# Seven transform tiles in the conv mixer, and an even layer that multiplies by a normalised operand

## The chip, the cores and the metric

The kernel runs on one core of a Trainium2 chip. The time is the device time of one execution in microseconds (us); lower is better. A core has a matrix engine (TensorE, PE in the rows; its weight loads are PEld), VectorE (DVE), ScalarE (ACT), GpSimd (POOL) and SyncE (SP), which issues the DMAs. Each engine works off its own instructions in program order and waits on semaphores for the others.

## The reference, cut to what matters

Four layers and two MLPs over 512 tokens of width 1024, in fp32. The change touches three of the stages.

```python
def conv_mixer(h, w_pw1, b_pw1, w_dw, b_dw, ln_g, ln_b, w_pw2, b_pw2):
    a = h @ w_pw1 + b_pw1
    u = a[..., :D_MODEL] * sigmoid(a[..., D_MODEL:])
    u = causal_depthwise_conv(u, w_dw) + b_dw          # 31 taps
    u = silu(layernorm(u, ln_g, ln_b))
    return u @ w_pw2 + b_pw2

def even_layer(x, norm_pre, norm_post, w_in, conv_w, conv_b, gate_w, gate_b, lam, sc_w, w_out):
    h = rmsnorm_2(x, norm_pre)
    xa, za, xb, gb, gc, zb = split(h @ w_in)           # six blocks of 1024 columns
    ua = centred_dwconv(xa, conv_w, 2) + conv_b        # 4 taps
    ya = rg_lru(ua, ..., False) + rg_lru(ua, ..., True)
    ya = ya * silu(za)
    yb = gb * centred_dwconv(gc * xb, sc_w, 1)         # 3 taps
    yb = yb * silu(zb)
    y = concatenate([ya, yb]) @ w_out
    return x + rmsnorm_2(y, norm_post)
```

The third is the start of the odd layer (`odd_layer`, gated linear attention): its decay gates are `log_sigmoid` of a product with a narrow low-rank projection.

## The kernel before, in words

**Layout.** Activations lie transposed: 8 tiles of 128 channels by 512 tokens (`h[:, k, :]`). Every product is made of three fp32r matmuls: an operand x is kept as XH (rounded) and XL = x - XH, a weight chunk of 128x1024 as `whi` and `wlo` likewise, and `mac` (L146 to L149) multiplies hi by XH, hi by XL and lo by XH. A *chunk* is one weight chunk against eight operand tiles, 24 matmuls into one PSUM bank.

**Weights.** `weights(ahead)` takes the next chunk and calls `split_to`, which for each chunk up to `ahead` further on issues a DMA on SP into one of four staging tiles, rounds it on ACT (`whi`, L101) and subtracts on the engine in `st["lo"]` (`wlo`, L102): DVE, except where the program sets POOL. It does so in the conv mixer from its first chunk on.

**Background work.** `chunk` calls `step` after every second k; `step` advances generators in the list `bg`, so that transforms, norms and recurrences are issued in slices between matmuls. What a generator issues stands in PE's, DVE's and ACT's queues in just that place.

**Conv mixer.** `a` is computed in 16 chunks: for each of the eight channel tiles m a gate chunk (`gate_half`) and a linear chunk (`lin_half`), which yields `u` (L749, L753). The first five m use all tokens; the last three are run in two halves of 256 tokens. The 31-tap convolution goes two ways. Tiles m < DIRECT (two) run `direct`: 31 instructions on DVE (L719, L721), a few per hook. The other six run `conv` once per half: three transposes on PE (`uT`, L676), a forward transform (`re`, L682), two products with the filter's spectrum on DVE (`pq`, L688), 12 inverse matmuls (`cv`, L696). YU, YA and YB say how many hooks lie between these steps. `centre` subtracts the mean of the first transform tile (`lns`) on DVE and adds sums on POOL (L664, L667). When all tiles of a half are done, `norm(half)` forms the layer norm (`lnm`), and `ln_a` to `ln_d` make XH and XL for the second product, `kouter2` (tile `ko`), one step per PACE[half] hooks.

**Even layer.** XZ is the order of the first 16 chunks (x is the recurrent branch, z its gate); then for each m the four chunks gc, xb, gb, zb. The operand is h times the gains `gfe`, without the norm's factor `rs2` (which `comb_a` and `comb_b` bring out of the sums while the first chunks run), so each result is multiplied by `rs2` behind its chunk: xa on DVE (L1077), za on DVE (L1084), the gc*xb product by `rq` = rs2 squared (L1101), yb on POOL (L1107), zb on DVE (L1121). `rg(m)` is the recurrence of tile m: `taps` (L975, L977), `halves`, four gate products, Tanh, Exp and Sqrt on ACT, two scans on DVE, and sums on POOL (L1022, L1028, L1049, L1050). It runs in the background, a step per half chunk pair, over all 48 chunks. Then `wob` and `woa` are the two halves of the output product.

**Odd layer.** `decays` (a generator) scales the low-rank projection, rounds it (`lrs`, L1331 to L1333), waits two hooks and issues the gate products `z` (L1343, L1344) between the chunks of `v`.

Of the kernel before, what the change touches and what calls it, by code (L numbers as in the profile page):

```python
# [7 lines left out]
F32 = mybir.dt.float32  # L8
F32R = mybir.dt.float32r
# [5 lines left out]
P = 128  # L15
NT = 512
# [31 lines left out]
def tile_model(ctx, tc, xT, wall, gwall, vecs, opost, wglr, bglr, wdw, dft, out):  # L48
# [14 lines left out]
    RGH, XAB, DCH, HDH, TKH, FIN = 0.5, 6, 2, 1.3, 1.5, 0.8  # L63
# [87 lines left out]
    def chunk(o, xh, xl, hook=0, wt=None, ks=range(KD), ns=slice(0, NT)):  # L151
# [465 lines left out]
    with ExitStack() as e:  # L617
# [51 lines left out]
        def conv(m, u, half, lag=0):  # L669
# [15 lines left out]
            for i in range(2):  # L685
                q = cp.tile([P, NW], F32, tag="pq", name="pq", bufs=4)
# [114 lines left out]
        PACE = (2, 1)  # L801
# [26 lines left out]
        st["lo"] = [pool]  # L828
        for c in range(10):
            m = c // 2  # L830
            if c == 7:
# [67 lines left out]
    with ExitStack() as e:  # L899
        ep = e.enter_context(tc.tile_pool(name="even", bufs=1))  # L900
        tmp_pool[:] = [ep, 6]
        sz = ep.tile([P, KD, NT], F32, name="sz")
        yb = ep.tile([P, KD, NT], F32, name="yb")
        rq = ep.tile([P, NT], F32, name="rq")
# [66 lines left out]
        def taps(m):  # L971
# [3 lines left out]
            dve.tensor_scalar(u, xa[:, 0:NT], vec[:, w0:w0 + 1], V("rcb", m), op0=ALU.mult, op1=ALU.add)  # L975
# [11 lines left out]
        def rg(m):  # L987
# [11 lines left out]
            for d in range(2):  # L999
                for g in range(2):  # L1000
# [6 lines left out]
                    s = gp.tile([P, NT], F32, tag="ri", name="ri", bufs=5)  # L1007
# [65 lines left out]
        def put_xa(m, o):  # L1073
# [3 lines left out]
            dve.tensor_tensor(out=xa[:, 2:NT + 2], in0=o, in1=rs2, op=ALU.mult)  # L1077
# [730 lines left out]
```

## Time and profile before

| | us |
|---|---|
| three runs | 1835.55, 1841.36, 5206.65 |
| their median | 1841.36 |
| the profiled execution | 1839.13 |
| its span, first to last instruction | 1837.4 |

| engine | busy us | share of the span |
|---|---|---|
| PE | 1790.3 | 97% |
| PEld | 1490.2 | 81% |
| DVE | 1036.1 | 56% |
| ACT | 795.9 | 43% |
| POOL | 519.1 | 28% |

PE is the engine that sets the time nearly everywhere: of the chain that ended last 80% lies on PE, 12% on DVE. The profile's forty slices show where it is not so: the row of PE has 8 in place of 9 in two neighbouring slices around 720 to 780 us, in one near 1400 us, and in the last third near 1580 us; in the row of the granted clock one slice (the second of the two in the conv mixer) has 8 in place of 9. To read the rows below: a row of the windows view gives for each engine its busy time and, in brackets, how many instructions it ran; PEclk is the mean clock that PE was granted, as a share of 2.4 GHz, the upper of its two levels (the lower is 1.2 GHz). In a row of the timeline the two first numbers are the start and the duration, xN says how many instructions in a row were merged, and the bracket at its end says how long the engine stood idle before it and for whom.

### The profile page before, as it was taken

Reading aid. Unit: us, or ns where it says so; the run is one execution under the profiler, and the core shown is the slowest. Engines: PE = TensorE matmul, PEld = TensorE weight load, DVE = VectorE, ACT = ScalarE, POOL = GpSimd, SP = SyncE. Lnnn points to the kernel's source line nnn. Section 1 sums busy time; section 2 is a strip of 40 time slices with the busy share of each in tenths; the row PEclk is TensorE's granted clock in tenths of the full one; section 3 lists DMA queues with packets and bytes.
Section 4 is the critical chain, followed back from the end, with each engine's and each line's share of the span. In section 5 each row is a group of like instructions: output and inputs, shape, how many; then the busy total and the mean of one; then the engine's idle time right before and its main releaser. Section 6 shows DMA issues by size and latency. Waiting matters only on the chain.

```text
span 1837.4 us, 22578 instructions
## 1 busy us (share of the span) xinstructions
PE 1790.3 (97%) x8762; PEld 1490.2 (81%) x8762; DVE 1036.1 (56%) x1457; ACT 795.9 (43%) x1234; POOL 519.1 (28%) x411
## 2 busy tenths in 40 slices
PE   9999999999999998899999999999998999999998
PEld 7778878888888877798888888888876878878887
DVE  5796544333334579865333334767878843745354
ACT  5334444332423433465332424545565644446553
POOL 1333322010202345535010201413434303552230
PEclk9999999999999999899999999999999999999999
DMA  5222113222223322112323223232222233222121
GB/s 189 69 80 73 59 54 103 95 99 96 93 100 101 101 73 91 46 47 81 98 94 101 91 98 104 80 115 101 84 80 92 81 103 103 70 87 81 47 69 47
DMA packets 45931, 159.68 MB, mean 87 GB/s; under 512 B 5217, under 2 KB 6625, under 8 KB 45824
## 3 DMA queue, kind: packets, MB, share of 16 engines
q1 hardware_dynamic: 45824, 158.24, 25.8%
q8 instruction: 69, 1.13, 0.3%
q14 instruction: 38, 0.31, 0.1%
HBM read 156.13 MB, written 2.10 MB: 86 GB/s over the span
## 4 chain that ended last, share of the span: by engine, by line
PE 80%; DVE 12%; ACT 4%; issue 2%; DMA 1%; POOL 1%; SPq 0%; DVEq 0%; ACTq 0%; POOLq 0%
PE w L148 12%; PE w L149 12%; PE w L147 12%; DVE y L721 2%; PE ko L148 1%; PE ko L149 1%; PE ko L147 1%; DVE wlo L102 1%; DVE ua L977 1%; PE k L147 1%; PE lg L467 1%; PE o L499 1%; PE v L441 1%; PE q L149 1%; PE q L147 1%
## 5 line engine op out<-in xcount | busy, mean ns | idle before, releaser
L102 DVE TENSOR_TENSOR wlo<-stg,whi 128x1024 fp32r<-128x1024 f32 x231 | 308.5, 1337 | 251.0 <-ACT whi L101 249.9
L101 ACT ACTIVATE whi<-stg 128x1024 fp32r<-128x1024 f32 x284 | 297.8, 1051 | 232.6 <-PE w L148 125.3
L596 POOL TENSOR_TENSOR UL<-u,UH 128x512 fp32r<-128x512 f32 x64 | 83.4, 1303 | 514.5 <-ACT UH L595 514.5
L148 PE MATMUL w<-XL,whi 128*128 128x512 f32 (+1 forms) x520 | 200.6, 386 | 0.0
L147 PE MATMUL w<-XH,whi 128*128 128x512 f32 (+1 forms) x520 | 200.6, 386 | 0.0
L149 PE MATMUL w<-XH,wlo 128*128 128x512 f32 (+1 forms) x520 | 200.6, 386 | 0.0
L148 PE MATMUL w<-UL,whi 128*128 128x512 f32 x512 | 199.4, 389 | 0.1
L147 PE MATMUL w<-UH,whi 128*128 128x512 f32 x512 | 199.2, 389 | 0.0
L149 PE MATMUL w<-UH,wlo 128*128 128x512 f32 x512 | 199.2, 389 | 0.0
L102 POOL TENSOR_TENSOR wlo<-stg,whi 128x1024 fp32r<-128x1024 f32 x53 | 130.7, 2473 | 158.7 <-ACT whi L101 158.4
L260 POOL TENSOR_TENSOR sacc<-sacc,sq 128x512 f32<-128x512 f32 (+1 forms) x57 | 71.2, 1256 | 181.2 <-ACT sq L259 180.9
L149 PEld LDWEIGHTS w<-XH,wlo 128*128 128x128 f32 x520 | 97.7, 188 | 19.7
L148 PEld LDWEIGHTS w<-XL,whi 128*128 128x128 f32 x520 | 97.7, 188 | 19.6
L147 PEld LDWEIGHTS w<-XH,whi 128*128 128x128 f32 x520 | 97.7, 188 | 19.6
L148 PEld LDWEIGHTS w<-UL,whi 128*128 128x128 f32 x512 | 96.1, 188 | 20.8 <-POOL UL L596 0.9
L149 PEld LDWEIGHTS w<-UH,wlo 128*128 128x128 f32 x512 | 96.1, 188 | 19.9
L147 PEld LDWEIGHTS w<-UH,whi 128*128 128x128 f32 x512 | 96.1, 188 | 20.0
L594 DVE TENSOR_TENSOR u<-relu 128x512 f32<-128x512 f32 x64 | 45.4, 710 | 104.5 <-ACT relu L592 104.5
L592 ACT ACTIVATE relu<-w 128x512 f32<-128x512 f32 x64 | 38.2, 597 | 151.0 <-PE w L149 151.0
L147 PE MATMUL ko<-XH,whi 128*128 128x256 f32 x256 | 74.4, 290 | 3.5 <-ACT XH L823 3.5
L604 DVE TENSOR_TENSOR acc<-w,acc 128x512 f32<-128x512 f32 x32 | 22.1, 692 | 97.1 <-PE w L149 97.1
L148 PE MATMUL ko<-XL,whi 128*128 128x256 f32 x256 | 73.7, 288 | 2.3 <-DVE XL L252 2.2
(469 smaller groups left out, 4201.1 us busy)
## 6 DMA issues: line engine op xcount, KB each, us to landing
stg<-wall SPq DMA_DIRECT2D x284, 512.0 KB, 3.3
gst<-gwall SPq DMA_DIRECT2D x4, 512.0 KB, 3.6
h<-xT SPq DMA_DIRECT2D x3, 512.0 KB, 5.8
out<-yo SPq DMA_DIRECT2D x6, 256.0 KB, 2.1
stg<-wall SPq DMA_DIRECT2D x8, 128.0 KB, 4.8
h<-xT SPq DMA_DIRECT2D x2, 256.0 KB, 3.8
ex<-wglr SPq DMA_DIRECT2D x2, 256.0 KB, 3.8
sacc<-opost SPq DMA_DIRECT2D x2, 256.0 KB, 4.4
```

Of the source, the lines that this page charges most:

```text
L101: act.activation(hi, src, AF.Copy)
L102: eng.tensor_tensor(out=lo, in0=src, in1=hi, op=ALU.subtract)
L147: pe.matmul(o, lhsT=hi[:, w], rhs=xh[:, k, ns], start=first, stop=False)
L148: pe.matmul(o, lhsT=hi[:, w], rhs=xl[:, k, ns], start=False, stop=False)
L149: pe.matmul(o, lhsT=lo[:, w], rhs=xh[:, k, ns], start=False, stop=last)
L260: eng.tensor_tensor(out=acc, in0=acc, in1=t, op=ALU.add)
L441: pe.matmul(acc[t], lhsT=XH[:, k, xs], rhs=wh, start=k == 0, stop=False)
L592: act.activation(r, o, AF.Relu)
L594: dve.tensor_tensor(out=u, in0=r, in1=r, op=ALU.mult)
L596: pool.tensor_tensor(out=UL[:, m, :], in0=u, in1=UH[:, m, :], op=ALU.subtract)
L604: dve.tensor_tensor(out=a, in0=o, in1=a, op=ALU.add)
L721: dve.scalar_tensor_tensor(o, src, w(j), o, op0=ALU.mult, op1=ALU.add)
```

## The change

- **Conv mixer.** DIRECT goes from 2 to 1: tile 1 is now a transform tile, and the pivot of `centre`. YB goes from (3, 3) to (4, 3): the inverse matmuls of the tiles m < 5 come one hook later; `pq` has six buffers in place of four. PACE goes from (2, 1) to (1, 1). The two settings of `st["lo"]` to POOL ahead of the second half are gone, so lo splits run on DVE until then. A new argument `mid` of `chunk` calls a function behind k = 3: the look-ahead split moves there from the chunk's start.
- **Even layer.** A new order SEQ; the first RAW = 7 chunks multiply by XH, XL as before. In the middle of chunks 3 to 6 `normal` makes NH, NL, the split of h*gfe*rs2, for two tiles each; all later chunks multiply by these, and their results need no rs2. The scalings listed above fall away with `rq` and `yb`; the first taps of both convolutions move from DVE to ACT; the sigmoid and product of z move from `rg` to the z chunk, the product from POOL to DVE. `do_b` splits each yb tile into XH, XL at once. Fewer buffers: xa 4 for 6, tmp 4 for 6, gate results 4 for 5, and the scans write in place.
- **Odd layer.** `decays` yields four times in place of two ahead of the `z` products.

```diff
-XZ = [("x", 0), ("x", 1), ("x", 2)] ...
+RAW = 7
+SEQ = [tuple(_s) for _s in ("x0 x1 x2 z0 z1 x3 z2 z3 z4 x4 z5 z6 z7 x5 g0 x6 g1 x7 " + " ".join(f"g{_m}" for _m in range(2, 8))).split()]
-    RGH, XAB, DCH, HDH, TKH, FIN = 0.5, 6, 2, 1.3, 1.5, 0.8
+    RGH, XAB, DCH, HDH, TKH, FIN = 0.5, 4, 2, 1.3, 1.5, 0.8
-    YU, YA, YB = (1, 1), (2, 3), (3, 3)
+    YU, YA, YB = (1, 1), (2, 3), (4, 3)
-    DIRECT, TG = 2, 0.6
+    DIRECT, TG = 1, 0.6
+            if mid and k == 3:
+                mid()
-        PACE = (2, 1)
+        PACE = (1, 1)
-        st["lo"] = [pool]
+        first_c = cur[0]
         for c in range(10):
             if c == 7:
-                st["lo"] = [pool]
-            chunk(o, XH, XL, hook="all" if c else 0, wt=weights(max(2, c - 4)))
+            chunk(o, XH, XL, hook="all" if c else 0, wt=weights(1 if c < 8 else 3), mid=lambda: split_to(first_c + c + max(2, c - 4)))
...
-            dve.tensor_scalar(u, xa[:, 0:NT], vec[:, w0:w0 + 1], V("rcb", m), op0=ALU.mult, op1=ALU.add)
+            act.activation(u, xa[:, 0:NT], AF.Identity, scale=vec[:, w0:w0 + 1], bias=V("rcb", m))
-            sg = tmp("sg")
-            act.activation(sg, sz[:, m, :], AF.Sigmoid)
-            pool.tensor_tensor(out=sz[:, m, :], in0=sz[:, m, :], in1=sg, op=ALU.mult)
-                hh = gp.tile([P, NT], F32, tag="hh", name="hh", bufs=2)
+                hh = si[d, 0]
+        def normal(ks):
+            ts = []
+            for k in ks:
+                ts.append(tmp("hn"))
+                dve.scalar_tensor_tensor(ts[-1], h[:, k, :], gfe[:, k:k + 1], rs2, op0=ALU.mult, op1=ALU.mult)
+            for k, t in zip(ks, ts):
+                act.activation(NH[:, k, :], t, AF.Copy)
+            for k, t in zip(ks, ts):
+                dve.tensor_tensor(out=NL[:, k, :], in0=t, in1=NH[:, k, :], op=ALU.subtract)
...
+        NORM = {3: (0, 1), 4: (2, 3), 5: (4, 5), 6: (6, 7)}
...
-            yield
-            yield
+            for _ in range(4):
+                yield
             tiles = [(t, d) for t in range(4) for d in (1, 0)]
```

How it moves instructions is shown at three places. On POOL, in the conv mixer between the zeroing of the direct tiles' padding (`ud`) and the first sums of `centre`, there stood before:

```order
L638 MEMSET ud_4770 128x30
L638 MEMSET ud_4771 128x30
L102 TENSOR_TENSOR wlo<-stg,whi 128x1024 x6
L752 MEMSET u 128x30
L102 TENSOR_TENSOR wlo<-stg,whi 128x1024 x3
L752 MEMSET u 128x30
L102 TENSOR_TENSOR wlo<-stg,whi 128x1024 x4
L752 MEMSET u 128x30
L102 TENSOR_TENSOR wlo<-stg,whi 128x1024
L664 TENSOR_TENSOR sacc_122<-sacc_122,y 128x256
```

and now:

```order
L638 MEMSET ud_4770 128x30
L752 MEMSET u 128x30 x3
L664 TENSOR_TENSOR sacc_122<-sacc_122,y 128x256
L667 TENSOR_TENSOR sacc<-sacc,sq 128x256
L664 TENSOR_TENSOR sacc_122<-sacc_122,y 128x256
```

The 14 splits that stood here, and two more further on, have left POOL. Of the 22 in the conv mixer six are left, all behind the start of the second half. They stand on DVE now. There, at the end of tile 4's linear chunk (`t` from `a` and `u` are L749 and L753; L721 is a tap; the half chunks begin behind it), there stood before:

```order
L688 TENSOR_TENSOR pq<-re,Wf_4765 128x384
L721 SCALAR_TENSOR_TENSOR y<-ud_4771,vec,y 128x512
L721 SCALAR_TENSOR_TENSOR y<-ud_4770,vec,y 128x512
L721 SCALAR_TENSOR_TENSOR y<-ud_4771,vec,y 128x512
L721 SCALAR_TENSOR_TENSOR y<-ud_4770,vec,y 128x512
L749 TENSOR_TENSOR t_5280<-a_5220,rs 128x512
L753 SCALAR_TENSOR_TENSOR u<-t_5280,vec,sg 128x512
```

and now:

```order
L721 SCALAR_TENSOR_TENSOR y<-ud_4770,vec,y 128x512
L100 TENSOR_TENSOR wlo<-stg,whi 128x1024 x2
L688 TENSOR_TENSOR pq<-re,Wf_4764 128x384
L688 TENSOR_TENSOR pq<-re,Wf_4765 128x384
L721 SCALAR_TENSOR_TENSOR y<-ud_4770,vec,y 128x512 x2
L749 TENSOR_TENSOR t_5308<-a_5258,rs 128x512
L753 SCALAR_TENSOR_TENSOR u<-t_5308,vec,sg 128x512
```

Half of the taps ahead of `u` are gone, and two splits stand farther ahead of it. The third place is DVE in the even layer from the moment that rs2 is known (the three scalings of xa), before:

```order
L1077 TENSOR_TENSOR xa<-xa,rs_120 128x512 x3
L102 TENSOR_TENSOR wlo<-stg,whi 128x1024
L975 TENSOR_SCALAR ua<-xa,vec 128x512
L977 SCALAR_TENSOR_TENSOR ua<-xa,vec,ua 128x512 x3
L298 TENSOR_TENSOR ual<-ua,uah 128x512
L1084 TENSOR_TENSOR sz<-za,rs_120 128x512
L102 TENSOR_TENSOR wlo<-stg,whi 128x1024
```

and now:

```order
L1087 TENSOR_TENSOR xa<-xa,rs_120 128x512 x3
L100 TENSOR_TENSOR wlo<-stg,whi 128x1024
L1055 SCALAR_TENSOR_TENSOR hn<-h,gfe,rs_120 128x512 x2
L1059 TENSOR_TENSOR NL<-hn,NH 128x512 x2
L976 SCALAR_TENSOR_TENSOR ua<-xa,vec,ua 128x512 x3
L298 TENSOR_TENSOR ual<-ua,uah 128x512
L1098 TENSOR_TENSOR zt<-za,rs_120 128x512
L1104 TENSOR_TENSOR sz<-zt,sg 128x512
L100 TENSOR_TENSOR wlo<-stg,whi 128x1024
```

In each of four chunks DVE gets four instructions of `normal` between two splits, and a product behind the sigmoid of z.

## Rows read from the trace of the kernel before

**Rows 1.** Windows: the conv mixer, and the middle part of it
```profile
637.00:797.00 160.00, 139.13 (x845) 121.87 (x844) 132.91 (x174) 65.67 (x117) 79.36 (x52) 0.95 0.23 77
658.00:758.00 100.00, 85.53 (x517) 75.44 (x515) 96.87 (x113) 30.45 (x54) 53.08 (x35) 0.95 0.20 69
```

**Rows 2.** Waits of 637 to 797 us: who waited for whom, total, times, longest
```profile
PE uT L676 <- DVE u L753: 13.6, 6, 4.9
PE ko L147 <- ACT XH L823: 3.5, 1, 3.5
```

**Rows 3.** Timeline around 670 us, DVE and POOL
```profile
666.56 5.66 DVE L721 SCALAR_TENSOR_TENSOR y<-ud,vec,y 128x512 f32<-128x512 f32 x2
669.10 2.58 POOL L102 TENSOR_TENSOR wlo<-stg,whi 128x1024 fp32r<-128x1024 f32 x1
...
679.08 1.41 DVE L721 SCALAR_TENSOR_TENSOR y<-ud,vec,y 128x512 f32<-128x512 f32 x2
```

**Rows 4.** Groups of 637 to 797 us: line, engine, shapes, count, busy, mean ns
```profile
L721 DVE SCALAR_TENSOR_TENSOR y<-ud,vec,y 128x512 f32<-128x512 f32 x60 | 66.6, 1153 | 0.1
L688 DVE TENSOR_TENSOR pq<-re,Wf 128x384 f32<-128x384 f32 x24 | 12.1, 546 | 0.5 <-PE re L682 0.5
L102 POOL TENSOR_TENSOR wlo<-stg,whi 128x1024 fp32r<-128x1024 f32 x22 | 55.6, 2533 | 52.0 <-ACT whi L101 51.8
```

**Rows 5.** Timeline of PE: one transform's parts and what follows each
```profile
673.83 0.52 PE L676 MATMUL uT<-ident,u 128*126 128x128 f32 x3 [3.01 <-DVE u L753]
674.10 0.48 PE L147 MATMUL a<-XH,whi 128*128 128x512 f32 x1
...
679.33 0.81 PE L682 MATMUL re<-uT,cd 126*128 126x384 f32 x2
679.68 0.69 PE L147 MATMUL a<-XH,whi 128*128 128x512 f32 x1
...
702.66 1.45 PE L696 MATMUL cv<-cd,pq 128*128 128x96 f32 x12
703.92 0.36 PE L147 MATMUL a<-XH,whi 128*128 128x256 f32 x1
```

**Rows 6.** Windows: even layer in four parts, and the decays
```profile
1180.00:1278.00 98.00, 97.55 (x440) 80.31 (x439) 66.75 (x94) 51.86 (x66) 24.24 (x31) 1.00 0.28 97
1278.00:1350.00 72.00, 70.65 (x308) 57.23 (x307) 60.77 (x62) 45.15 (x59) 27.88 (x22) 1.00 0.28 96
1350.00:1420.00 70.00, 63.91 (x267) 50.57 (x266) 55.80 (x59) 38.75 (x52) 25.41 (x18) 0.98 0.23 76
1420.00:1526.00 106.00, 104.93 (x460) 85.74 (x459) 70.62 (x80) 56.44 (x76) 23.27 (x19) 1.00 0.28 95
1627.00:1650.00 23.00, 21.00 (x76) 14.36 (x74) 10.34 (x13) 11.42 (x19) 12.72 (x12) 0.85 0.32 109
```

**Rows 7.** Groups of 1180 to 1526 us, the lines that are changed
```profile
L102 DVE TENSOR_TENSOR wlo<-stg,whi 128x1024 fp32r<-128x1024 f32 x56 | 72.5, 1297 | 19.3 <-ACT whi L101 19.1
L975 DVE TENSOR_SCALAR ua<-xa,vec 128x512 f32<-128x512 f32 x8 | 13.5, 1683 | 0.0
L1101 DVE TENSOR_TENSOR cpad<-gx,rq 128x512 f32<-128x512 f32 x8 | 6.7, 833 | 0.3
L1131 DVE SCALAR_TENSOR_TENSOR h<-h,vec,rs 128x512 f32<-128x512 f32 x8 | 6.0, 744 | 0.0
L1104 DVE TENSOR_SCALAR yb<-cpad,vec 128x512 f32<-128x512 f32 x8 | 3.9, 486 | 4.2 <-POOL cpad L1100 3.7
L297 ACT ACTIVATE uah<-ua 128x512 fp32r<-128x512 f32 x8 | 5.1, 632 | 48.3 <-DVE ua L977 48.3
```

**Rows 8.** Timeline around 1405 us: the longest wait of the even layer
```profile
1409.23 0.80 PE L149 MATMUL gc<-XH,wlo 128*128 128x512 f32 x1 [3.32 <-DVE wlo L102]
```

**Rows 9.** Timeline of the decays: the low part of the projection, then the first `z`
```profile
1635.65 1.62 DVE L1333 TENSOR_TENSOR lrs<-sacc,lrs 32x512 fp32r<-32x512 f32 x1 [0.70 <-ACT lrs L1332]
1637.33 0.50 PE L1343 MATMUL z<-wg,lrs 128*128 128x512 f32 x1 [1.94 <-DVE lrs L1333]
```

More of the change, by code (lines that the diff above doesn't have):

```diff
@@ L149, in mac, with chunk @@
         pe.matmul(o, lhsT=lo[:, w], rhs=xh[:, k, ns], start=False, stop=last)
-    def chunk(o, xh, xl, hook=0, wt=None, ks=range(KD), ns=slice(0, NT)):
+    def chunk(o, xh, xl, hook=0, wt=None, ks=range(KD), ns=slice(0, NT), mid=None):
         hi, lo = wt or weights()
@@ L685, in conv @@
             for i in range(2):
[L686 removed]
+                q = cp.tile([P, NW], F32, tag="pq", name="pq", bufs=6)
                 w = Wf[i][:, m * P - WC:(m + 1) * P - WC][:, None, :].to_broadcast([P, 3, P])
@@ L1053, in tile_model, with do_xa @@
         gate_load(0)
-        def do_xa(m):
-            o = psum("mm", "xa")
-            chunk(o, XH, XL, hook=RGH)
-            xaw.append((m, o))
+        def normal(ks):
[7 more added lines that the diff above has]
+                dve.tensor_tensor(out=NL[:, k, :], in0=t, in1=NH[:, k, :], op=ALU.subtract)
+        def do_xa(m, raw, mid):
+            o = psum("mm", "xa")
+            if raw:
+                chunk(o, XH, XL, hook=RGH, mid=mid)
+            else:
+                chunk(o, NH, NL, hook=RGH)
+            xaw.append((m, o, raw))
             if m == 0:
@@ L1076, in put_xa, with do_za, do_b @@
             pool.memset(xa[:, NT + 2:], 0.0)
-            dve.tensor_tensor(out=xa[:, 2:NT + 2], in0=o, in1=rs2, op=ALU.mult)
+            if raw:
+                dve.tensor_tensor(out=xa[:, 2:NT + 2], in0=o, in1=rs2, op=ALU.mult)
+            else:
+                act.activation(xa[:, 2:NT + 2], o, AF.Copy)
             xas[m] = xa
             bg.append(rg(m))
-        def do_za(m):
+        def do_za(m, raw, mid):
             o = psum("mm" if m else "a", "za")
-            chunk(o, XH, XL, hook=RGH)
-            dve.tensor_tensor(out=sz[:, m, :], in0=o, in1=rs2, op=ALU.mult)
+            if raw:
+                chunk(o, XH, XL, hook=RGH, mid=mid)
+                t = tmp("zt")
+                dve.tensor_tensor(out=t, in0=o, in1=rs2, op=ALU.mult)
+                o = t
+            else:
+                chunk(o, NH, NL, hook=RGH)
+            sg = tmp("sg")
+            act.activation(sg, o, AF.Sigmoid)
+            dve.tensor_tensor(out=sz[:, m, :], in0=o, in1=sg, op=ALU.mult)
             zas.add(m)
-        for kind, m in XZ:
-            (do_xa if kind == "x" else do_za)(m)
-        for m in range(8):
+        cvs = [sacc, sacc2]
+        def do_b(m):
             o = psum("mm", "gc")
-            chunk(o, XH, XL, hook=RGH)
+            chunk(o, NH, NL, hook=RGH)
             gcs = tmp("gc")
@@ L1094, in tile_model @@
             o = psum("mm", "xb")
-            chunk(o, XH, XL, hook=RGH)
-            pr = tmp("gx")
-            dve.tensor_tensor(out=pr, in0=o, in1=gcs, op=ALU.mult)
+            chunk(o, NH, NL, hook=RGH)
             cpad = ep.tile([P, NT + 2], F32, tag="cpad", name="cpad", bufs=2)
@@ L1721, in _layout @@
     w = f("even_w_in_2")[0]
-    for kind, m in XZ:
-        c = (0 if kind == "x" else 1024) + m * P
-        cols(w, c, c + P)
-    for m in range(8):
-        for base in (4096, 2048, 3072, 5120):
+    for kind, m in SEQ:
+        for base in {"x": (0,), "z": (1024,), "g": (4096, 2048, 3072, 5120)}[kind]:
             cols(w, base + m * P, base + (m + 1) * P)
```

62 lines of the change are left out of this document (27 added, 35 removed).

## Prediction

> **What bounds the kernel now.** I read the page's engine table first (PE 97%), then the windows of the stages that the diff touches, then who waits there, then the timeline at the waits. In the windows the reader should subtract: a stretch's length less PE's busy time is PE idle; the share missing from PEclk, times the length, is about what matmuls at the lower clock cost on top. The conv mixer, 160 us long, has PE busy for 139.13, so 20.9 idle, and a granted clock of 0.95, so 0.05 x 160 = 8.0 more: 28.9 lost [rows 1]. The even layer's four stretches have 0.45 + 1.35 + 6.09 + 1.07 = 9.0 idle, and the third a clock of 0.98 (0.02 x 70 = 1.4): 10.4 lost. The 23 us around the decays have 2.0 idle and a clock of 0.85 (3.45): 5.45 lost [rows 6]. That is 44.7 us; everywhere else in these stages PE works through, and no edit can bring more than 44.7 except by removing matmuls, which none does.
>
> Whom PE waits for: in the conv mixer six waits for DVE's `u` make 13.6, one for ACT's XH 3.5 [rows 2]; the other 20.9 - 13.6 - 3.5 = 3.8 are small ones. In the middle 100 us DVE is busy for 96.87 and PE for 85.53 [rows 1]: there DVE sets the pace, not PE. Part of DVE's time is not work: two taps took 5.66 us while a split ran on POOL from 669.10, and 1.41 some us later without one [rows 3]. The mean over 60 taps is 1.153, and the 22 POOL splits take 2.533 each [rows 4]. So the timeline says that a tap costs 0.7 alone and up to 2.8 beside a POOL split.
>
> **Conv mixer.** On DVE, 30 of 60 taps go, and the other 30 should fall towards 0.7: 66.6 becomes 30 x 0.7 = 21, a gain of 45.6. Sixteen splits come to DVE, at 1.30 (the even layer's row of L102 [rows 7]): +20.8. The extra tile has two halves of two products: 4 x 0.546 = +2.2 [rows 4]. Net -22.6; were all of it in the middle stretch, DVE would be busy for 96.9 - 22.6 = 74 us. What PE needs there is 85.5, less the 5 us of lower clock in it (0.05 x 100), plus the new tile. That tile's price I read from the matmuls that stand right behind its parts: the next matmul starts 0.27 after `uT`, 0.35 after `re`, 1.26 after `cv` [rows 5], so 1.88 a half and 3.8 for two. PE then needs about 84, more than DVE's 74: DVE stops setting the pace.
>
> What stays lost: `u` can still be late at the ten places where a transform directly follows its `u` (four early tiles, three late ones twice), since at the second order place two splits and a tap or two still stand ahead of it. Bounds: nothing, or the 13.6 of before; I take 0.5 each, 5, as with 74 of 84 us busy a queue of one or two instructions is what a new one finds. Of the wait for XH and the small waits (7.3) I take 5: PACE (1, 1) lets the first half's norm steps come at every hook, which brings XH earlier, but its operands still come through DVE and ACT. YB one hook later gives `pq` more time, and six buffers keep it from blocking; both cost PE nothing, since other chunks' matmuls fill the hook. Of the clock 1: it reads 1.00 in the two even stretches with at most 1.35 us idle [rows 6]. Left 5 + 5 + 1 = 11; gain 28.9 - 11 - 3.8 = **14.1** (5 to 23 by the bounds of `u`, the clock going with it).
>
> The mid-chunk call brings a new wait: DVE's `wlo` waits for ACT's `whi`, with `pq`, `t` and `u` queued behind it and PE's `cv` and `uT` waiting for those. It looks ahead by at least one chunk, so PE itself doesn't ask for the split; the wait is inside the 0.5 per `u`. SP's DMAs move by half a chunk, and nothing else on that queue is time-critical then. I take nothing for them.
>
> **Even layer.** DVE loses eight first taps (13.5), eight products with `rq` (6.7), eight scalings of zb, eight first taps of yb (3.9) and, with xa and za, one more; it gains 16 instructions of `normal`, priced by the nearest row, 0.744: 11.9 [rows 7]. With the scalings of zb at the same 0.744, that is 13.5 + 6.7 + 6.0 + 3.9 - 11.9, about -18 of the 254 us that DVE is busy [rows 6]. POOL loses 17 products. The longest wait here is 3.32 of a `gc` matmul for DVE's `wlo` [rows 8]; DVE being late is the cause, so less on DVE and POOL should take most of the 6.09.
>
> Whether the first taps should move to ACT is where the row decides: `ua`'s took 1.683 on DVE, yb's, the same operation on the same shape, 0.486, and ACT's 128x512 rounding 0.632 [rows 7]. So it isn't the tap that is dear but what runs beside it. The Trainium skill's "ScalarE: Activation LUTs", section "Rules for kernel authors", says to use VectorE and not ScalarE for multiply and add, which speaks against this part. By that rule's direction at the undisturbed prices the 16 taps cost 16 x (0.632 - 0.486) = 2.3 us more, and the sum would end at 1816 were all of it on the path; by the rows DVE is rid of 17.4 and ACT has room.
>
> The new wait: PE must find the normalised tiles at chunk 7. A chunk is 24 matmuls at 97.55/440 = 0.222 [rows 6], 5.3 us; from the end of the third chunk PE reaches tile 6 of chunk 7 after 4.75 chunks, 25.3 us. DVE from the same point (the third order place and its three repeats) has 4 splits (5.2) and 28 others at 0.744 (20.8), 26.0; NL waits for ACT's NH, between nothing (hidden by the pair's other tile) and 4 x 0.63 = 2.5; I take 1.2. So 27.2 against 25.3: a stall of 2, between 0.7 and 3.2. I leave 2.6 of other waits, about the 1.07 + 1.35 that the calmer stretches show. Gain 10.4 - 4.6 = **5.8** (2 to 9).
>
> Fewer buffers and scans in place make a gate's sigmoid wait for the scan of the tile before; recurrences run in the background a tile apart, so I take nothing. `do_b` splits each tile at once, eight roundings spread over the layer where seven stood in the last chunk; nothing on the path.
>
> **Odd layer.** The `z` matmul waited 1.94 for DVE's `lrs`, whose last step took 1.62 [rows 9]. Two more hooks put 12 matmuls of `v` ahead of `z`, 12 x 0.222 = 2.7 us: the wait is covered, and with it the clock stays up. Left 0.4: **5.0** (2 if the clock falls anyway).
>
> **The sum.** 14.1 + 5.8 + 5.0 = 24.9. Against the profiled execution's own 1839.13: **1814**. The median of the runs shown, 1841.36, is 2.2 above that; about 2% is what a measurement of this kernel can tell from no change, so faster means below 1804.5 and slower above 1878.2.
>
> **Rivals.**
> *DVE stays late in the conv mixer.* If the taps' length doesn't come from POOL's splits, the 30 left still take 1.153: DVE's gain is 34.6 - 20.8 - 2.2 = 11.6, and it is busy 85 of the 84 to 89 us that PE needs. For it: centre's sums stay on POOL, and six splits too. Against: the 1.41 beside the 5.66 [rows 3]. The waits for `u` and the rest then stay at the 20.9 of now, less 1: 20, with no lower clock. Conv gains 5.1; **1823**; chance 0.20.
> *The normalised operand is late.* If each pair waits for two NHs in full behind ACT's queue, 4 x 1.26 = 5.0, DVE ends at 31, 5.7 behind PE, and the even gain is used up: **1820**; 0.12. Against: ACT is busy 52 of the first 98 us [rows 6].
> *Nearly all stalls go.* Without saturation `u` is there in time and the clock stays up everywhere: 44.7 - 3.8 less 3 that stay, 38: **1801**; 0.12. For it: PE's idle 0.45 in the even layer's first 98 us, where DVE is busy 68% [rows 6].
> *ACT becomes the bound of the recurrences (slower).* ACT gets eight NH, four xa and 16 first taps, 28 x 0.632 = 17.7 on top of the 192 us of 346 [rows 6], 2.2 per tile, and every recurrence is a chain through ACT. If that chain has no slack, PE waits for its gates at each tile. From 24.9/8 = 3.1 us per tile the gain is gone; at 5, the time is 1839 - 25 + 40 = **1854**; 0.06. Against: ACT's rounding of `ua` waited 48.3 us in sum for DVE's taps [rows 7], so DVE, not ACT, is the late one.
>
> My forecast's own chance is 0.50, its range 1805 to 1822. The range for 8 in 10 is 1802 to 1828: it takes in the first two rivals and leaves out most of the third, the fourth and a little of the tails. Faster by over 2% is the third rival and the lower tail, 0.15; slower 0.02, the fourth from 8 us per tile; the rest, 0.83, within 2%.
>
> **What would show it.** Conv mixer: the window of its middle with DVE well under 85% and PE over 93%; L721 30 times at 0.7 to 0.9; six POOL splits; waits for `u` under 6 in sum. If L721 stays at 1.1, the first rival holds. Even layer: no wait above 3 us at the chunk that first reads NH and NL, under 5 us idle in all, no ACT releaser at the head of PE's waits. Decays: no wait for `lrs`, clock 1.00. My forecast is wrong if the waits for `u` come back in other places (ahead of the half chunks above all, where three tiles are transformed twice), or if a `wlo` on DVE is late for PE, which no row of POOL's splits could show.

## The result, and the profile after

The changed kernel takes 1815.88 us in the median of four runs (1815.21 to 1816.9), the kernel before beside it 1839.32. The ratio is 0.988, with a 95% interval of 0.9859 to 0.9901: 18 to 26 us faster. The forecast was 1814, within 1802 to 1828, with 0.83 for a change of less than 2%. (One of the four executions of the kernel before took 5206.65 us; the ratio leaves it out, the median 1839.32 has it in and would be 1837.29 without it.) So the sum came out. Its terms did not all do so: two of them missed by about as much in opposite directions, and a second measurement of the same changed kernel, below, gave 1819.29. That the sum is only 2 us off is luck.

First the page of the changed kernel: the engines' busy time, and the forty slices of PE and of its clock.

```profile
PE 1785.0 (98%) x8796; PEld 1490.1 (82%) x8796; DVE 979.1 (54%) x1430; ACT 815.7 (45%) x1267; POOL 442.5 (24%) x380
PE   9999999999999999999999999999999999999998
PEclk9999999999999999999999999999999999999999
PE 88%; DVE 5%; ACT 3%; issue 2%; DMA 1%; POOL 0%; SPq 0%; DVEq 0%; ACTq 0%; POOLq 0%
```

No slice of PE but the last has an 8 any more, and of the chain that ended last 5% lies on DVE where it was 12%. Now the windows, laid as [rows 1] and [rows 6] were: the conv mixer, its middle, four parts of the even layer, the decays. Columns as there: PE, PEld, DVE, ACT and POOL busy with their instructions, PEclk, DMA share, GB/s.

```profile
639.50:789.50 150.00, 140.52 (x874) 123.14 (x873) 99.68 (x162) 68.20 (x121) 38.70 (x36) 0.95 0.24 80
656.00:748.00 92.00, 89.19 (x572) 78.86 (x570) 68.12 (x103) 33.68 (x60) 20.26 (x23) 1.00 0.25 81
1173.00:1271.00 98.00, 97.16 (x439) 80.23 (x438) 74.01 (x109) 65.47 (x88) 18.82 (x24) 1.00 0.29 99
1271.00:1343.00 72.00, 72.00 (x317) 59.27 (x316) 49.71 (x54) 48.39 (x65) 22.30 (x23) 1.00 0.30 100
1343.00:1411.00 68.00, 65.53 (x287) 53.38 (x286) 49.66 (x55) 42.49 (x57) 16.00 (x15) 1.00 0.27 86
1411.00:1508.00 97.00, 97.00 (x429) 80.20 (x428) 52.89 (x60) 53.00 (x68) 9.61 (x10) 1.00 0.28 94
1608.00:1631.00 23.00, 22.76 (x95) 16.28 (x94) 13.42 (x16) 14.34 (x24) 12.90 (x12) 1.00 0.36 117
```

In the middle of the conv mixer DVE is busy for 68 of 92 us, where it was 97 of 100, and PE stands idle for 2.8 us there. But the whole mixer still has a clock of 0.95, the same as before. The even layer has 3.3 us of idle in all, and two of its four parts have none. Whom PE waited for in the conv mixer (total, times, longest, in us):

```profile
PE uT L676 <- DVE u L753: 4.5, 4, 2.0
PE ko L145 <- ACT XH L823: 2.4, 1, 2.4
PE ko L146 <- DVE XL L825: 1.6, 1, 1.6
PE wf L652 <- DMA y<-wdw: 0.8, 1, 0.8
```

The waits for `u` went from 13.6 to 4.5 [rows 2]. In the even layer three waits are left; these two stand at its longest stop:

```profile
PE gc L145 <- ACT whi L99: 1.4, 1, 1.4
PE gc L147 <- DVE wlo L100: 1.1, 1, 1.1
```

And the groups that answer to [rows 4]:

```profile
L721 DVE SCALAR_TENSOR_TENSOR y<-ud,vec,y 128x512 f32<-128x512 f32 x30 | 23.7, 789 | 0.3
L100 DVE TENSOR_TENSOR wlo<-stg,whi 128x1024 fp32r<-128x1024 f32 x16 | 19.7, 1242 | 18.4 <-ACT whi L99 18.4
L688 DVE TENSOR_TENSOR pq<-re,Wf 128x384 f32<-128x384 f32 x28 | 14.2, 549 | 2.2 <-PE re L682 2.2
L100 POOL TENSOR_TENSOR wlo<-stg,whi 128x1024 fp32r<-128x1024 f32 x6 | 14.5, 2429 | 13.6 <-ACT whi L99 13.6
```

Thirty taps at 0.789, sixteen splits at 1.242, 28 products, six splits left on POOL: each count is as forecast, and each duration that was forecast (0.7, 1.30 and 0.546) came within 0.1 us.

Where the 22.2 us between the two profiled spans (1837.4 and 1815.2) lie, from the first matmul of one stage to the first of the next:

| stage | before | after | gain | forecast |
|---|---|---|---|---|
| all ahead of the conv mixer | 629.4 | 631.0 | -1.6 | 0 |
| conv mixer | 201.6 | 192.7 | 8.9 | 14.1 |
| the MLP behind it | 349.4 | 349.4 | 0 | 0 |
| even layer to its first `wob` | 299.9 | 291.2 | 8.7 | 5.8, with `wob` |
| `wob` | 45.5 | 43.5 | 2.0 | |
| `woa` | 45.8 | 44.8 | 1.0 | none |
| `v` with the decays | 37.6 | 33.7 | 3.9 | 5.0 |

The rows add up to 22.9; 0.7 is lost behind them. The conv mixer gave 5 less than forecast, the even layer with `wob` 10.7 in place of 5.8, and `woa` gave 1.0 that no term had.

### The profile page after: what moved, and what is told of

The parts are those of the page before. It is cut to its first block, busy times and chain, and to the rows that moved or that the text cites. A ratio compares the mean times of both kernels' runs of the same rounds, so it can differ in the third digit from the quotient of the medians.

```text
span 1815.2 us, 22602 instructions
## 1 busy us (share of the span) xinstructions
PE 1785.0 (98%) x8796; PEld 1490.1 (82%) x8796; DVE 979.1 (54%) x1430; ACT 815.7 (45%) x1267; POOL 442.5 (24%) x380
## 4 chain that ended last, share of the span: by engine, by line
PE 88%; DVE 5%; ACT 3%; issue 2%; DMA 1%; POOL 0%; SPq 0%; DVEq 0%; ACTq 0%; POOLq 0%
PE w L146 12%; PE w L147 12%; PE w L145 12%; PE ko L146 2%; PE ko L147 2%; PE ko L145 1%; PE a L145 1%; PE a L147 1%; PE a L146 1%; PE k L145 1%; PE lg L467 1%; PE o L499 1%; ACT whi L99 1%; PE v L441 1%; PE q L147 1%
## 5 line engine op out<-in xcount | busy, mean ns | idle before, releaser
L100 DVE TENSOR_TENSOR wlo<-stg,whi 128x1024 fp32r<-128x1024 f32 x247 | 328.5, 1332 | 267.5 <-ACT whi L99 266.4
L100 POOL TENSOR_TENSOR wlo<-stg,whi 128x1024 fp32r<-128x1024 f32 x37 | 89.6, 2428 | 122.1 <-ACT whi L99 121.9
L146 PEld LDWEIGHTS w<-UL,whi 128*128 128x128 f32 x512 | 96.1, 188 | 20.9 <-POOL UL L596 1.0
```

What stands on the lines that cost most here:

```text
L100: eng.tensor_tensor(out=lo, in0=src, in1=hi, op=ALU.subtract)
L146: pe.matmul(o, lhsT=hi[:, w], rhs=xl[:, k, ns], start=False, stop=False)
```

## The experiments

Twelve kernels ran, in three groups of four; the kernels of a group shared one chip and its runs of the kernel before (medians 1834.9, 1837.8 and 1836.0). A ratio is always to those, and kernels of different groups are compared by it. Names that begin with b_ are the kernel before with one part of the change done; those that begin with a_ are the changed kernel with something undone or added.

### What the conv mixer's parts are worth

**The lo splits back on POOL (a_pool_lo).**

```diff
         first_c = cur[0]
+        st["lo"] = [pool]
```

> The changed kernel with one part undone: the lo splits of the conv mixer's first half (16 of 22) are back on POOL. Theory A (a POOL split holds up DVE instructions that read two SBUF operands, so moving the splits is what freed DVE): the mean of L721 goes from 0.79 back above 1.0, waits for u grow, 1819 to 1825 us against 1815.9. Rival B (the halved taps are what freed DVE; a split costs DVE 1.25 where it stands and about 2 of stretch where it doesn't, and there is room for either): 1815 to 1817, waits for u as now (4.5).

Measured: 1819.58, ratio 0.9922 (0.9903 to 0.9942). The taps are back at more than 1.1, as theory A had it (row of the groups):

```profile
L721 DVE SCALAR_TENSOR_TENSOR y<-ud,vec,y 128x512 f32<-128x512 f32 x30 | 35.0, 1165 | 0.3
```

and of the stage as a window, here and in the changed kernel:

```profile
630.00:825.20 195.20, 183.67 (x1198) 164.91 (x1197) 127.67 (x202) 92.25 (x166) 93.89 (x74) 0.97 0.21 70
631.00:823.70 192.70, 183.22 (x1198) 164.44 (x1197) 127.81 (x218) 92.11 (x166) 53.80 (x58) 0.96 0.22 71
```

Yet DVE's busy time over the stage is 127.7, against 127.8 in the changed kernel: what the splits cost DVE by holding it up is what they cost by standing on it, as rival B said. Waits for `u` were 6.4 in place of 4.5. The time is in theory A's range, not in rival B's. By the ratios it is 3 us above the second measurement of the changed kernel (0.9904; the intervals overlap) and 8 above the first (0.988; they do not). So each theory has one half right: the move of the splits is worth some 2 us of waits, and in time 0 to 8.

**Two direct tiles again (a_direct2).**

```diff
-    DIRECT, TG = 1, 0.6
+    DIRECT, TG = 2, 0.6
```

> The changed kernel with two direct tiles in place of one: 30 more taps at about 0.75 on DVE (+22 us), one transform tile less on PE (-3.8). Theory A: taps stay at 0.8, DVE has about 90 of 94 us, so waits for u come back in part: 1816 to 1822. Rival B: DVE is saturated again as before, 1824 to 1830.

Measured: 1826.45, ratio 0.9962 (0.9946 to 0.9979). The taps stay at 0.818, but there are 60 again; DVE is busy for 90.67 of the 110 us from 654 to 764, and PE waits (a window, then the waits):

```profile
654.00:764.00 110.00, 98.82 (x566) 86.43 (x565) 90.67 (x133) 35.31 (x60) 21.24 (x20) 0.92 0.21 67
```

```profile
PE uT L676 <- DVE u L753: 11.2, 6, 2.5
```

Time as rival B had it, taps as theory A had them. By the ratios it is 11 us slower than the second measurement of the changed kernel and 15 slower than the first. Part of that is clock: the stage's share was 0.91 in this profile, but the profiled execution (1830.55) is one of the two slowest of six, so how much of it is clock in the others is not shown.

**The splits alone (b_dve_lo).**

```diff
         sgs = {}
-        st["lo"] = [pool]
...
-                st["lo"] = [pool]
```

> The kernel before with one part done: the lo splits of the conv mixer's first half on DVE, all else as it was (60 taps). Theory A: taps fall to about 0.8 (-22 us), splits add about 20, but no DVE instruction is held up any longer (the others lost some 10): DVE gains, the time is 1831 to 1836 against 1839.3. Rival B: 60 taps and 16 splits on DVE are more than it has room for: 1839 to 1848.

Measured: 1839.05 against 1834.89, ratio 1.0017 (1.0003 to 1.0032): no gain, a loss of 1 to 6 us. Rival B. The taps fell to 0.839 as theory A said, but the waits only changed their name:

```profile
PE cv L696 <- DVE pq L688: 9.0, 5, 4.1
PE uT L676 <- DVE u L753: 5.3, 5, 1.6
PE ko L147 <- ACT XH L823: 3.5, 1, 3.5
```

A split on DVE that waits for ACT's `whi` has `pq` queued behind it, which it had not while it stood on POOL. This run has the splits without the mid-chunk call, the later YB and the six `pq` buffers that go with them in the change; the splits with those, but with two direct tiles, are a_direct2.

**The direct tile alone (b_direct1).**

```diff
-    DIRECT, TG = 2, 0.6
+    DIRECT, TG = 1, 0.6
```

> The kernel before with one part done: one direct tile in place of two (splits still on POOL, lags as they were). Theory M (the tile that goes is the main part of the conv mixer's gain): waits for u fall from 13.6 to 6 to 8, 3.8 is paid on PE, 3 to 7 us faster than the kernel before. Rival N (splits on POOL and fewer taps only work together): within 2 us of the kernel before.

Measured: 1826.68 against 1836.02, ratio 0.9947 (0.9931 to 0.9964): 9 to 10 us faster (7 to 13 by the interval) from one number. Waits for `u` are 2.9, fewer than in the changed kernel, with all 22 splits on POOL and the taps at 1.189. The windows are the whole stage and its middle, then the waits:

```profile
629.50:819.50 190.00, 180.57 (x1199) 161.73 (x1198) 131.17 (x202) 91.69 (x166) 94.80 (x74) 0.99 0.22 72
654.00:748.00 94.00, 90.97 (x583) 80.41 (x583) 71.05 (x91) 34.27 (x62) 53.75 (x39) 1.00 0.23 79
```

```profile
PE ko L147 <- ACT XH L823: 3.4, 1, 3.4
PE uT L676 <- DVE u L753: 2.9, 3, 1.9
```

The stage is 190.0 us long, shorter than the 192.7 of the full change. Theory M, and more than it asked. The other edits of the conv mixer (splits, mid-chunk call, YB, PACE, buffers) together add nothing to its length that these two profiles can tell from zero. Undone in the changed kernel (a_direct2) the tile was worth 11 to 15, so it is the main part in either order.

**No direct tile at all (a_direct0).**

```diff
-    DIRECT, TG = 1, 0.6
+    DIRECT, TG = 0, 0.6
```

> The changed kernel with no direct tile: the last 30 taps (23.7 us of DVE) become an eighth transform tile (3.8 us of PE, 4 pq of 0.55 on DVE). Theory E (DVE is no longer the bound; with 69 of 94 us busy the remaining waits for u, 4.5, come from the order of single instructions): waits for u fall by at most 3, the tile costs 3.8, so 0 to 3 us slower than the unaltered kernel beside it. Rival F (each tap that goes is worth what it was worth from two tiles to one): 5 us or more faster.

Measured: 1817.09 (0.989, 0.9876 to 0.9905), beside 1819.29 for the unaltered changed kernel: the intervals overlap. Waits for `u` fell from 4.6 to 2.3, and PE's busy time over the stage rose by 3.7 (186.88 for 183.22 us), which is the price of a tile that the prediction read as 3.8. This is theory E by its mechanism; in time nothing that can be told, so the step from two tiles to one is not repeated.

### What the clock does

**The changed kernel once more (after_again).** No edit.

> The changed kernel once more, unaltered, as the yardstick of the three runs beside it: every theory expects 1813 to 1818 us.

Measured: 1819.29 (1816.1 to 1823.42), ratio 0.9904 (0.9885 to 0.9923), 3.4 us above its first median. The waits of the profiled execution are those of the first (4.6 for `u`, 2.4 and 1.6 for XH and XL, 0.8 for `wdw`), but for 0.8 in place of 0.2 for `pq`. The stage is 7.4 us longer. Windows of the stage, and of two places in it:

```profile
629.70:829.80 200.10, 189.88 (x1198) 168.70 (x1197) 128.50 (x218) 92.22 (x166) 53.72 (x58) 0.93 0.21 69
640.00:660.00 20.00, 19.23 (x58) 12.44 (x57) 4.51 (x6) 7.38 (x10) 0.00 (x0) 0.74 0.19 67
772.00:785.00 13.00, 10.50 (x51) 9.77 (x52) 11.25 (x24) 8.92 (x19) 5.65 (x5) 0.61 0.24 83
```

The clock fell to its lower level behind the wait for `wdw` (0.8 us, the 0.74 row) and behind a 2.0 us wait for `u` (0.79 from 690 to 706 us), where it had not in the first execution, and behind the waits of `ko` (the 0.61 row), where it had. So the same program with nearly the same waits gives a conv mixer of 192.7 or 200.1 us. The stage's length times its granted clock takes most of that out (the clock is given to 0.01, which is about 1 us). Three kernels below left the conv mixer's code as it was, and show how far two executions of one stage still differ in this column, by 2 to 2.5:

| kernel | stage us | clock | product | waits for `u` |
|---|---|---|---|---|
| before | 201.6 | 0.96 | 193.5 | 13.6 |
| the same stage in b_even_nopool | 206.3 | 0.95 | 196.0 | 14.6 |
| b_dve_lo | 200.9 | 0.97 | 194.9 | 5.3 (and 9.0 for `pq`) |
| b_direct1 | 190.0 | 0.99 | 188.1 | 2.9 |
| after | 192.7 | 0.96 | 185.0 | 4.5 |
| after_again | 200.1 | 0.93 | 186.1 | 4.6 |
| the same stage in a_taps_dve | 196.8 | 0.95 | 187.0 | 4.5 |
| the same stage in a_yield2 | 193.0 | 0.96 | 185.3 | 4.5 |
| a_pool_lo | 195.2 | 0.97 | 189.3 | 6.4 |
| a_direct2 | 206.8 | 0.91 | 188.2 | 11.2 |
| a_direct0 | 193.7 | 0.96 | 186.0 | 2.3 |
| a_dve_lo2 | 195.1 | 0.96 | 187.3 | 6.0 (and 3.1 for `pq`) |
| a_early | 195.6 | 0.96 | 187.8 | 7.2 (and 3.6 for `pq`) |
| a_early_d0 | 201.8 | 0.94 | 189.7 | 5.0 (and 3.4 for `pq`) |

By this column the direct tile is worth 5 on the kernel before (193.5 to 188.1), and the rest of the conv mixer's edits 1 to 3. The other order gives the reverse: all the rest without the tile (a_direct2, 188.2) is 5 below the kernel before, and the tile adds 1 to 3. So with the clock taken out either part brings most of the gain by itself; it is in the timed runs that the tile outweighs the rest. That the difference is how often the clock falls fits the profiles (17, 3 and 37 us at the lower clock in the conv mixers of before, b_direct1 and a_direct2), but there is one profile of each.

**All splits of the conv mixer on DVE (a_dve_lo2).**

```diff
                 bg.append(norms[0])
-                st["lo"] = [pool]
```

> The changed kernel with the six last POOL splits of the conv mixer on DVE too. Theory C (the half clock from 765 to 779 us, 6.8 us of it lost, follows from the waits for XH and XL at the start of ko, and these from DVE instructions held up by four POOL splits, 0.42 to 2.6 each): waits for XH and XL under 1.5 in sum, half clock at most 3.4 us long there, 1806 to 1811 us. Rival D (DVE pays for the splits itself and PE gets its XH no earlier): 1814 to 1818, half clock still there.

The reason for it is a piece of the changed kernel's timeline where `ko` begins: DVE's instructions beside POOL's remaining splits.

```profile
753.34 2.30 DVE L753 SCALAR_TENSOR_TENSOR u<-t,vec,sg 128x256 f32<-128x256 f32 x1 [0.63 <-ACT sg L743]
755.56 2.60 DVE L658 TENSOR_TENSOR y<-y,sS 128x256 f32<-128x256 f32 x1
752.98 4.89 POOL L100 TENSOR_TENSOR wlo<-stg,whi 128x1024 fp32r<-128x1024 f32 x2 [8.66 <-ACT whi L99]
762.91 2.35 POOL L100 TENSOR_TENSOR wlo<-stg,whi 128x1024 fp32r<-128x1024 f32 x1 [2.95 <-ACT whi L99]
763.57 1.97 DVE L825 TENSOR_TENSOR XL<-z,XH 128x256 fp32r<-128x256 f32 x1 [1.41 <-ACT XH L823]
```

Measured: 1819.28, ratio 0.9918 (0.9901 to 0.9935). The waits for XH and XL did go (0.6 and none), but `pq` and `u` were late in their place, and the clock of that part was 0.79:

```profile
PE uT L676 <- DVE u L753: 6.0, 3, 3.1
PE cv L696 <- DVE pq L688: 3.1, 3, 2.0
```

```profile
750.00:790.00 40.00, 33.10 (x207) 30.95 (x206) 25.44 (x56) 23.79 (x47) 6.11 (x8) 0.79 0.20 66
```

Theory C has its first half right and falls by the second. The time is 1 us above rival D's range and so no gain, as D had it, though not for D's reason: the waits for XH and XL did shrink.

**The norm earlier, the last split later (a_early), and so without a direct tile (a_early_d0).**

```diff
-            for _ in range(3):
+            for _ in range(3 if half else 2):
                 yield
...
             yield
-            yield
+            if half:
+                yield
...
-                if half and c:
+                if half and 0 < c < 5:
                     split_to(c0 + 17 + c)
```

> The changed kernel with the first half's norm two hooks (1.4 us) earlier and the last split of the second half put off until ko's first k is issued: ACT's whi (1.04) no longer stands ahead of the first XH, nor a POOL split beside the first XL. Theory O (these two set the 4.0 us that ko waits): waits for XH and XL fall under 1.5 in sum, no half clock of 13.7 us behind them: 3 to 9 us faster than the unaltered changed kernel (1816 to 1819). Rival P (another operand is late next, as when those splits went to DVE): within 2 us of it.

> The same two edits, and no direct tile. Theory O and E together: waits for u under 3, for XH and XL under 1.5; 1808 to 1815 us. Rival P: 1815 to 1819.

Measured: 1820.52 (0.9914, 0.9898 to 0.9931) and 1819.7 (0.9912, 0.9896 to 0.9928). No wait for XH or XL is left in either, and in a_early this stands in its place:

```profile
PE uT L676 <- DVE u L753: 7.2, 4, 3.7
PE cv L696 <- DVE pq L688: 3.6, 1, 3.6
```

Rival P: four us of waits taken from one operand came back on two others (`u` from 4.6 to 7.2, `pq` from 0.8 to 3.6). Three kernels took these four us away, and none became faster.

### The even layer and the decays

**POOL's products on DVE (b_even_nopool).** Kernel before, two `pool.tensor_tensor` (silu of z, yb times rs2) made `dve.tensor_tensor`.

> The kernel before, with the two products of the even layer that POOL made (silu of z, yb times rs2, 16 instructions, 30.3 us of POOL) on DVE instead, at about 0.7 each: +11 us there. Theory K (POOL's products hold up DVE's taps, and taking them from POOL is the main gain of the even layer): taps fall from 1.41 and 1.68 to under 1.1, that stage loses 2 to 6 us, time 2 to 6 us under the kernel before. Rival L (the gain comes from the instructions that go altogether; eleven more on DVE make wlo later still): same or up to 5 us slower.

Measured: 1835.51 against 1836.02, ratio 1.0002 (0.9989 to 1.0016). The taps fell (to 0.903 and 1.191; theory K had both under 1.1), and DVE's busy time over the stage stayed as it was (255.0 for 253.9):

```profile
L977 DVE SCALAR_TENSOR_TENSOR ua<-xa,vec,ua 128x512 f32<-128x512 f32 x24 | 21.7, 903 | 1.0
L975 DVE TENSOR_SCALAR ua<-xa,vec 128x512 f32<-128x512 f32 x8 | 9.5, 1191 | 0.0
```

```profile
1180.00:1526.00 346.00, 338.69 (x1478) 276.55 (x1477) 254.96 (x313) 195.27 (x253) 70.42 (x74) 0.99 0.27 93
```

```profile
PE gc L149 <- DVE wlo L102: 5.2, 2, 4.0
```

The long wait for `wlo` stayed. Rival L by the time ("same or up to 5 us slower"): moving POOL's products to DVE brings nothing. The run does not test what freeing POOL is worth when the products go altogether, as most do in the change. DVE's busy time, 254 before and 226 after, is one difference that is left; the order of the chunks, the work moved to ACT and the early split of each tile are others, and no run has any of them alone. So which edit the even layer gained by is not shown.

**The first taps back on DVE (a_taps_dve).** Changed kernel, `act.activation` of both first taps made `dve.tensor_scalar` as before.

> The changed kernel with the 16 first taps of the even layer back on DVE, as it was before. Theory G (the prediction's: beside POOL's work a tap on DVE is dear, and what DVE gave away there is part of the gain): 1 to 4 us slower than the unaltered kernel, L975-like taps above 0.8 in the mean. Rival H (with POOL's products gone the tap costs 0.49 to 0.55 on DVE and 0.75 on ACT, so it doesn't matter or DVE is the better place): within 1 us.

Measured: 1817.69 (0.9897, 0.9882 to 0.9911), beside 1819.29 unaltered. Rival H by the time: where the taps stand can't be told. The rows are between the theories:

```profile
L974 DVE TENSOR_SCALAR ua<-xa,vec 128x512 f32<-128x512 f32 x8 | 10.6, 1330 | 0.0
```

```profile
PE gc L147 <- DVE wlo L100: 2.6, 1, 2.6
```

The eight taps of `ua` are dear on DVE (1.330; ACT takes 0.806 for them), as theory G expected, those of the short convolution are not (0.749 for 0.723). One wait for `wlo` grew from 1.1 to 2.6, and one of 1.4 for `whi` went: in the changed kernel ACT's first tap of the short convolution stands ahead of that `whi`, and had waited 2.7 for its input. The timed runs show nothing of it.

**Two yields in the decays (a_yield2).**

```diff
-            for _ in range(4):
+            for _ in range(2):
                 yield
```

> The changed kernel with two yields ahead of z in decays in place of four. Theory I (the two hooks cover the wait of 1.94 and keep the clock up): 2 to 5.5 us slower than the unaltered kernel, the wait of z for lrs back, half clock behind it. Rival J (the wait had gone anyway, since other work moved, or POOL's products no longer lie beside lrs): within 1 us.

Measured: 1819.11 (0.9904, 0.9887 to 0.992), beside 1819.29 unaltered: no difference. The wait is back,

```profile
PE z L1357 <- DVE lrs L1347: 1.9, 1, 1.9
```

and the `v` stage took 34.6 us for 33.7 and 33.2; but the waits of `cum` behind it, 1.0 and 0.3 in the changed kernel, are gone, and the clock did not fall. Of theory I the wait came true and the half clock did not; the time is rival J's: about 1 us in the stage, of which about half is given back behind it.

## Why the prediction was right, and where it was not

**The sum was right because two errors cancelled.** It said 24.9; the spans differ by 22.2. The stages give 8.9 + 8.7 + 2.0 + 1.0 + 3.9 = 24.5, less 1.6 ahead of the conv mixer, where in that execution the clock fell once at 11 us, and 0.7 at the end. But conv mixer and even layer are each some 5 off.

**Conv mixer, 14.1 forecast, 8.9 measured: the term for the clock.** DVE's sum held (74 us of the middle 100 forecast, 68 of 92 measured; over the whole stage it fell by 30.5, from 158.3 to 127.8, where 22.6 was forecast), and with it the claim that DVE stops setting the pace. What was to stay idle was 10; the window has 150 - 140.52 = 9.5. Waits for `u` were to be 5; they are 4.5. The tile's 3.8 was 3.7 by a_direct0. "Of the clock 1" failed: the stage kept 0.95, 7.5 us. The step behind it took the clock of stretches with under 1.4 us of idle in 72 or 98 us as what a sum of waits cut in half would give. It is not the sum that matters: a_direct0, with 6.8 us of idle in its conv mixer, had 13.7 us at the lower clock there, and the kernel before, with 20.9, had 17.1. Each fall to the lower level in the conv mixers of the fourteen traces begins in a wait of PE, or soon behind one or two close together, of 0.7 to 4.9 us, however little is idle elsewhere (not every such wait has a fall: one of 3.0 for `u` in the kernel before had none). The waits at the start of `ko` were left in place by the change: they were in the rows [rows 2], 3.5 for XH, and became 2.4 + 1.6. That PACE (1, 1) would bring XH earlier was a hope and not a reading.

**Why the stage is faster was put on the wrong part.** The prediction took the POOL splits for half of the cause, from the row with two taps in 5.66 [rows 3]. That row is right as a mechanism. DVE instructions with two operands in SBUF are held up beside a split; the products `pq`, with one of their operands in PSUM, are not, in the same stretch of the kernel before (min/median/max in ns):

```profile
L721 DVE SCALAR_TENSOR_TENSOR y<-ud,vec,y x60: 733/743/2926, 653.2 to 749.1; 128x512 f32<-128x512 f32 x60
L688 DVE TENSOR_TENSOR pq<-re,Wf x24: 539/546/558, 678.1 to 788.0; 128x384 f32<-128x384 f32 x24
```

The Trainium skill's "SBUF — State Buffer", section "Who interferes with whom", says just this: a VectorE instruction with two SBUF inputs contends with a GpSimd instruction that reads SBUF, one with at most one such input, outside what the Trainium skill calls the 2-port perf modes, does not. The trace agrees, 2926 against 558; 11 of the 24 products ran beside POOL's work. The first taps of `ua` in the even layer (L975) read only one tensor in SBUF and are held up all the same: the one that ran undisturbed took 0.540, the seven beside POOL's work 1.5 to 2.7. Whether they run in such a mode no run here shows. But a split that is moved to DVE takes 1.24 there, about what it took by holding DVE up: DVE's busy time with the splits on POOL (a_pool_lo, 127.7) and on DVE (127.8) is the same. In the prediction's own sum this could be seen: -45.6 for the taps is 30 x 0.7 for those that go (21) and 25 for the stretch, and the splits cost 20.8. The stretch and the splits nearly pay for each other; the tile is what is left. The timed runs show it: the tile alone 9 to 10 us (b_direct1) and undone 11 to 15 (a_direct2), the splits alone nothing (b_dve_lo) and undone 0 to 8 (a_pool_lo).

The first rival (DVE stays late, 1823) is out by the page, with taps at 0.789, though its premise, taps at 1.15, came true in b_direct1 without the lateness: with DVE busy for 71 of 94 us even stretched taps come in time. The third (nearly all stalls go, 1801) is out by the conv mixer's 9.5 us of idle and its clock.

**Even layer, 5.8 forecast, 10.7 measured: what was lost before was read too small.** Two terms. What stays idle is 0.84 + 0 + 2.47 + 0 = 3.3, forecast 4.6. And the loss of before was more than idle plus lower clock (10.4): the same matmuls kept PE busy for 337.0 of 346 us before and for 331.7 of 335 after, so 5.4 us of loss stood inside PE's busy time. Some 1.7 of it is lower clock (3.4 us long, from the 0.80 us matmul of [rows 8] on, where most take 0.39); some is in matmuls that start right behind a wait and run long at full clock (about 0.50 us; eleven waits in the layer before and three after). Subtracting busy time from a window gives a lower bound of the loss, so "no edit can bring more than 44.7" did not follow. DVE's busy time fell by 28 in this layer, where 18 was forecast; that this is the cause is argued, not shown. At the longest stop the trace does show what went: before, `wlo` stood behind the product with `rq` and the first tap on DVE and PE waited 3.3; now the product is gone, the tap stands on ACT ahead of `whi`, and PE waits 1.4 for `whi` and 1.1 for `wlo`. The sign "no ACT releaser at the head of PE's waits" thus failed, in the layer that did better than forecast. `wob`'s 2.0 is a part that the prediction passed over with "nothing on the path": its waits for XH and XL (0.6 and 0.5 in that profile) are gone with the tiles split one by one. `woa`'s 1.0 nobody looked for; it lies outside the rows that the term was made of and stands below. This gain varies too: in after_again, where the clock fell once in the layer for 3.4 us, the two stages took 336.0 us in place of 334.7.

The stall of 2 at the first chunk that reads NH and NL did not come. DVE's list took 27.6 us (1193.91 to 1221.49), forecast 27.2. PE came later than forecast, since gate products of a recurrence lie between the chunks: it began chunk 7 at 1217.93, 24 us behind the start of that list, not 21, and reached tile 6 four us later.

```profile
1193.91 1.88 DVE L1087 TENSOR_TENSOR xa<-xa,rs 128x512 f32<-128x512 f32 x3
1218.69 1.40 DVE L1055 SCALAR_TENSOR_TENSOR hn<-h,gfe,rs 128x512 f32<-128x512 f32 x2
1220.14 1.35 DVE L1059 TENSOR_TENSOR NL<-hn,NH 128x512 fp32r<-128x512 f32 x2
1217.93 0.39 PE L145 MATMUL za<-NH,whi 128*128 128x512 f32 x1
```

NL followed hn without an idle gap in each of the four: ACT's NH was hidden. So the second rival is out, and with one us to spare. The fourth (ACT as the bound, slower) is out as well: two of the four parts have no PE idle, with ACT busier by 17 us in the layer (209.4 for 192.2).

**The first taps.** The Trainium skill's "ScalarE: Activation LUTs", section "Rules for kernel authors", puts multiply and add on VectorE. The prediction weighed that against the 1.683 beside POOL. By the rows of a_taps_dve the mixer's taps are dearer on DVE (1.330 for 0.806) and the short convolution's are equal (0.749 for 0.723). The prediction said that by the rule the sum would end 2 us later; the runs show no difference either way (1817.69 with the taps on DVE, 1819.29 with them on ACT). Nothing that PE waits for hangs on these taps for more than 1.5 us.

**Odd layer, 5.0 forecast, 3.9 measured in the stage, about 1 by experiment.** The wait for `lrs` went, as forecast. The other 3 us were the lower clock behind it, 6.8 us long in the profile of before. That comes in some executions only: of the five traces in which `z` waits 1.9 to 2.0 for `lrs`, the clock fell behind the wait in three (6.8 us in before and b_even_nopool, 3.4 in b_direct1) and stayed up in b_dve_lo and a_yield2; in the nine without the wait it never fell there. So the forecast's "with it the clock stays up" holds, but this pair of profiles counts one of the longest falls, and the timed runs of a_yield2 show no loss. And a cost was left out: the `cum` products, whose place did not move, now wait 1.3.

## What to carry to other kernels

Moving work from an engine that blocks another onto the blocked one is worth only the difference between the two; add both before counting a gain, and look at the work that simply goes away. Here a DVE busy all the time and one with a quarter of its time free differed much, and more freedom beyond that brought nothing: after the first direct tile, taking off the second freed 19 us of DVE and brought no time that can be told, and taking away the splits or the norm's wait moved the waits to another operand. And where a profile shows the lower clock, take its cost from several executions of the same program before giving it to an edit: here one program's conv mixer was 192.7 or 200.1 us long.

No kernel tried was told apart from the changed one as faster. The runs point to one that was not tried: the conv mixer of b_direct1 with the even layer of the change; by the stages' lengths it would save the 192.7 - 190.0 = 2.7 us between the two profiles, less than executions of one program differ, and by the column with the clock taken out it would cost 1 to 3.

## What was not expected of the hardware

The first `wf` product waits for its DMA at about 645 us. In six of the fourteen traces 3.4 or 10.2 us at the lower clock follow, in after_again behind a wait of 0.8 us; in the first execution of the same program it waited 0.8 as well, and the clock stayed up. Of the eight traces in which this wait is 0.7 to 1.0 us six have the fall, of the six in which it is 0.5 or less none. A wait of 2.0 for `u` was likewise followed by a fall in the one and not in the other. What decides it is open.

The `woa` products of 512 columns take 0.233 us each from start to start in the four traces with the old even layer, and 0.227 in the ten with the new one; with those of 256 columns (0.120 and 0.118) that makes the stage 1.0 us shorter, at full clock and with no wait. What changed for them is the tile that their moving operand lies in (BH and BL of their own before, NH's and NL's place after). In the groups of PE the same shows as 394 ns busy for one product before and 389 after. Whether the place is the cause was not tested.
